# A hybrid decoder layer on one core: the feed-forward weight blocks multiplied in narrower pieces of columns

## The chip, the cores and the metric

One core of a Trainium2 chip runs the whole layer in one launch. The metric is device microseconds of that core for one execution, from the first to the last instruction with the launch around it; a small number is good. The core has a matrix engine (PE), whose weight loads are recorded as a row of their own (PEld), a vector engine (DVE), a scalar engine (ACT), a general engine (POOL) and a queue that issues transfers (SP).

## The reference

One decoder layer on 512 tokens of width 1024, all in float32: a half-step SwiGLU feed-forward block, a mixer, a second feed-forward block of the same shape, and a last normalisation. The change touches only the two feed-forward blocks. With `h` the normalised and modulated input (512 x 1024) each of them computes

```
x = x + 0.5 * gate * ((silu(h @ w_gate) * (h @ w_up)) @ w_down)
```

with `w_gate` and `w_up` of 1024 x 2816 and `w_down` of 2816 x 1024. The mixer between them (a gated convolution beside sparse attention, with one input and one output projection) is computed by the same helper, but at widths that the change leaves alone.

## The kernel before, in words

**Layout.** Everything is kept transposed: a tile has 128 channels on the partitions and the 512 tokens along the columns. `DK` = 8 tiles make the model width, `FK` = 22 tiles the hidden width, taken in two halves of `FH` = 11.

**Three products for one.** A float32 matrix is split into a high part and a low part, both in the engine's fast float32 form (`whi`, `wlo` for weights, `hhi`, `hlo` for the input, `ghi`, `glo` for the hidden layer). A product of a 128 x 128 block of weights with a 128 x 512 tile is three passes: high weights by high input, high weights by low input, low weights by high input. `mm3` (line 280) writes these. Where tile and bank are 512 wide it does the columns in `HALVES`, two pieces of 256: the three passes on the first half, then the three on the second. So one step of one block is six matmuls of 256 columns. Every matmul in the instruction stream brings its own weight load of 128 x 128.

**The feed-forward stage.** `ffn` (line 586) runs `main` (line 637) once for each block. The first three hidden tiles (`GRP` = 3) are computed by `first_group` or `first_products`, by halves of the tokens, as the input is built. For each of the other 19 hidden tiles `project` (line 542) is called twice, once for the gate block and once for the up block: 8 steps each, accumulated in one bank of 512 columns. Then `glu` (line 599) applies the gate with ACT and DVE and splits the result into `ghi`, `glo`. After the first 11 hidden tiles `part` (line 617) multiplies the down blocks of the first half: 8 output tiles of 11 steps over all 512 columns. After the last 11 hidden tiles come 6 output tiles of 11 steps over all columns, and then the last two output tiles by halves of the tokens, so that the normalisation behind them can begin early; in these the bank slice is 256 wide.

**The order of the work.** A planner written in the kernel (`Plan`) puts the instructions of all engines in order when the program is built. Each step tells it an estimated time: `c_mm3(T)` for a full step of `project` and of `part`. The order on each engine is then fixed in the program, and semaphores hold it together. Weights come over the SP queue in units of 512 KB into four buffers (`raw`), ACT makes the high part (line 372) and DVE or POOL the low part (line 361). During the first feed-forward block the same queue also brings the conditioning matrix (`araw`), which DVE sums (line 871); a few small matmuls of PE reduce those sums in `ada_reduce`.

**Elsewhere.** In the mixer `project` computes 14 blocks of the input projection in halves. The attention has matmuls of other widths with the same 128 x 128 loads: `scores` (line 1311 on) multiplies query tiles with keys of 128 to 512 columns, first with all 128 rows (`ks,q`) and then with 64 (`kl,q`); `compressed` multiplies query tiles with 64 columns (`kcs,q`).

Of the kernel before, what the change touches and what calls it, by code (L numbers as in the profile page):

```python
# [20 lines left out]
T = 512  # L21
D = 1024
DK = D // P
F = 2816
FK = F // P
FH = FK // 2
# [109 lines left out]
class Plan:  # L136
# [12 lines left out]
    def go(self, rank, task):  # L149
        self.n += 1  # L150
        self.step([rank, self.n, task, [self.at], None], None)
# [8 lines left out]
    def give(self, slots, i, at=None):  # L160
        slots.idle.append((*(at or self.at), i))
        able = [w for w in slots.waiters if w[4] < len(slots.idle)]
        if able:
            w = min(able, key=lambda w: w[:2])
            slots.waiters.remove(w)
            self.step(w, self.take(slots, w))
# [52 lines left out]
def c_act(n):  # L219
    return ACT, 0.1 + 0.84e-3 * n  # L220


def c_tt(n):
    return DVE, 0.07 + 1.04e-3 * n


def c_stt(n):
    return DVE, 0.13 + 1.04e-3 * n
# [14 lines left out]
def c_mm3(n):  # L243
    return PE, 3 * max(n / 2370, 0.105)
# [11 lines left out]
def tile_hymba_layer(ctx: ExitStack, tc: tile.TileContext, xT, pos, cols_d, con_d, wa0, wa1, f1a, f1b, f1d,  # L256
# [9 lines left out]
    HALVES = (slice(0, T // 2), slice(T // 2, T))  # L266

    bank_of = [ps.tile([P, T], F32, name=f"b{i}") for i in range(8)]
# [8 lines left out]
    def mm(o, lhsT, rhs, start, stop):  # L277
        nc.tensor.matmul(o, lhsT, rhs, start=start, stop=stop)  # L278

    def mm3(o, w, x_, start, stop):  # L280

        n = o.shape[-1]
        wide = n == T and x_[0].shape[-1] == T
        halves = HALVES if wide else (slice(0, n),)
        for ts in halves:
            x0, x1 = (x_[0][:, ts], x_[1][:, ts]) if wide else x_
            o_ = o[:, ts] if wide else o
            mm(o_, w[0], x0, start and ts is halves[0], False)
            mm(o_, w[0], x1, False, False)
            mm(o_, w[1], x0, False, stop and ts is halves[-1])  # L290


    col = const.tile([P, N_COLS], F32, name="col")
# [84 lines left out]
    def take_unit():  # L378
        used[0] += 1
        return used[0] - 1  # L380

    def cols(u, j, n=P):
        i = w_at[u]
        return whi_of[i][:, j * n:(j + 1) * n], wlo_of[i][:, j * n:(j + 1) * n]

    def free_unit(u):
        give(slots_of.get(u, ws), w_at[u])
# [128 lines left out]
    def h_of(d, ts=FULL):  # L516
        return hhi[d][:, ts], hlo[d][:, ts]
# [17 lines left out]
    def residual(d, b, gate, ts, norm):  # L535
        n = ts.stop - ts.start
        yield c_stt(n)
        nc.vector.scalar_tensor_tensor(x[d][:, ts], bank_of[b][:, ts], gate, x[d][:, ts], op0=OP.mult, op1=OP.add)  # L538
        give(banks, b)
        yield from norm.add(d, ts)  # L540

    def project(b):

        u = take_unit()
        yield made[u]
        for d in range(DK):
            yield c_mm3(T)
            mm3(bank_of[b], cols(u, d), h_of(d), d == 0, d == DK - 1)
        free_unit(u)

    def start_builds(s, norm):
# [15 lines left out]
    def first_group(order, built, accs, end, n_cols=2 * GRP):  # L567

        uses = {}
        for n, (i, d) in enumerate(order):  # L570
            yield built[i, d]
            if d not in uses:
                uses[d] = take_unit()
            yield made[uses[d]]
            ts = HALVES[i]
            for j in range(n_cols):
                if n == 0:
                    accs[j] = yield banks
                yield c_mm3(T // 2)
                mm3(bank_of[accs[j]][:, ts], cols(uses[d], j), h_of(d, ts), n == 0, n == len(order) - 1)  # L580
            if i == 1:
                free_unit(uses[d])
        done(end)


    def ffn(s, gp, accs, norm, end):
        ghi = [gp.tile([P, T], F32R, name=f"ghi{k}") for k in range(FH)]
        glo = [gp.tile([P, T], F32R, name=f"glo{k}") for k in range(FH)]
        sg_of = [gp.tile([P, T], F32, name=f"sg{k}") for k in range(2)]
        for k in range(KEEP[s]):  # L590
            whi_of.append(gp.tile([P, UNIT], F32R, name=f"whik{k}"))
            wlo_of.append(gp.tile([P, UNIT], F32R, name=f"wlok{k}"))
            give(kept[s], len(whi_of) - 1)
        sgs, gs = Slots(range(2)), [Slots([k]) for k in range(FH)]
        g_in = [Event() for _ in range(FK)]
        gate = [mod[:, 3 * s + 2, d:d + 1] for d in range(DK)]
        at = {}

        def glu(f, bg, bu):
            k = yield sgs  # L600
            yield c_act(T)
            nc.scalar.activation(sg_of[k], bank_of[bg], AF.Silu)
            give(banks, bg)
            q = yield scr
            yield c_tt(T)
            nc.vector.tensor_mul(scr_of[q], sg_of[k], bank_of[bu])  # L606
            give(banks, bu)
            give(sgs, k)
            j = yield gs[f % FH]
            yield c_act(T)  # L610
            nc.scalar.activation(ghi[j], scr_of[q], AF.Copy)  # L611
            yield c_tt(T)
            nc.vector.tensor_sub(glo[j], scr_of[q], ghi[j].bitcast(F32))  # L613
            give(scr, q)
            done(g_in[f])

        def part(half, d, b, ts, keep=False):
            for k in range(FH):
                n = d * FH + k
                if (half, n // 8) not in at:  # L620
                    at[half, n // 8] = take_unit()
                u = at[half, n // 8]
                yield made[u]
                yield g_in[half * FH + k]
                yield c_mm3(ts.stop - ts.start)
                mm3(bank_of[b][:, ts], cols(u, n % 8), (ghi[k][:, ts], glo[k][:, ts]), k == 0, k == FH - 1)
                if n % 8 == 7 and not keep:
                    free_unit(u)
                if half == 0 and d == DK - 1:
                    give(gs[k], k)  # L630

        def first_half(d, b):
            yield c_stt(T)
            nc.vector.scalar_tensor_tensor(x[d], bank_of[b], gate[d], x[d], op0=OP.mult, op1=OP.add)
            give(banks, b)

        def main():
            for f in range(GRP):
                go(R_GLU, glu(f, accs[2 * f], accs[2 * f + 1]))
            for f in range(GRP, FK):  # L640
                if f == FH:
                    for d in range(DK):
                        b = yield banks
                        yield from part(0, d, b, FULL)
                        if d == 0:
                            yield mod_in[3 * s + 2]
                        go(R_X, first_half(d, b))
                bg = yield banks
                yield from project(bg)
                bu = yield banks  # L650
                yield from project(bu)
                go(R_GLU, glu(f, bg, bu))
            for d in range(DK - 2):
                b = yield banks
                yield from part(1, d, b, FULL)
                go(R_X, residual(d, b, gate[d], FULL, norm))
            for ts in HALVES:
                for d in (DK - 2, DK - 1):
                    b = yield banks
                    yield from part(1, d, b, ts, True)  # L660
                    go(R_X, residual(d, b, gate[d], ts, norm))
            for n in range(8, FH):
                free_unit(at[1, n])
            done(end)

        go(R_MAIN, main())


    start = ctx.enter_context(ExitStack())
# [298 lines left out]
    with ExitStack() as mixer:  # L968
# [620 lines left out]
        def fill():  # L1589
            for n, f in enumerate(FILL):  # L1590
                if f == "val":
                    yield from value_products()
                elif f == "cmp":
                    yield from compressed_hidden()
                else:
                    b = yield banks.spare(FILL_SPARE)
                    yield from project(b)
                    receive(f, b, scr, n)
            done(h_done)
# [3 lines left out]
        n = 0  # L1603
# [295 lines left out]
```

## Time and profile before

| | |
|---|---|
| Time of the runs shown | median 1066.27 us of three (1066.21, 1066.27, 1082.69) |
| The profiled execution's own time | 1077.18 us |
| Its span, first to last instruction | 1075.4 us |
| PE busy | 1054.2 us, 98% of the span, 8753 matmuls and 8753 weight loads |
| DVE, ACT, POOL busy | 606.0, 408.7, 51.2 us |
| Granted PE clock, mean | 0.991 of full speed |
| Read from HBM | 130.14 MB |

The profile comes from one execution; its own time is 10.9 us over the median of the runs. A matmul's recorded time is the time from its start to its modelled end, and matmuls overlap, so the time that one takes from the engine is read from the distance between the starts of two that follow each other, or from their number in a stretch of time. The first feed-forward block lies between 24 and 409 us of the span (its down blocks at 164 to 228 and 348 to 409 us), the mixer between 409 and 697 us, the second feed-forward block from there to 1066 us (down blocks at 815 to 877 and from 1002 us).

### The profile page before, as it was taken

What the parts mean: (1) busy time and instruction counts of PE and PEld (TensorE: products, weight loads), DVE (VectorE), ACT (ScalarE), POOL (GpSimd) and SP (SyncE); (2) the same over time, 40 slices, a digit from 0 to 9 for tenths busy, and PEclk for the clock granted to TensorE, in tenths of its full rate; (3) what the DMA queues carried; (4) which work ended last, traced back from release to release, by engine and by line L of the source; (5) the groups of instructions that cost most, each with busy time, mean ns of one, the idle gap of its engine ahead of it and who ended that gap; (6) DMA issues with size and microseconds to landing.
All of it is one profiled execution on the core that took longest, in us unless ns stands there. A gap on an engine that the chain in (4) does not pass through costs nothing.

```text
span 1075.4 us, 20561 instructions
## 1 busy us (share of the span) xinstructions
PE 1054.2 (98%) x8753; PEld 1009.8 (94%) x8753; DVE 606.0 (56%) x1069; ACT 408.7 (38%) x713; POOL 51.2 (5%) x47
## 2 busy tenths in 40 slices
PE   8999999999999999999999999999999999999997
PEld 5899999999999999998887789999999999999997
DVE  4988888833333347699787786744333333233334
ACT  4552222222222224458566775333222122222321
POOL 0310100000000001021001010000000000000000
PEclk8999999999999999999999999999999999999999
DMA  9669999422232231344201014133233322322202
GB/s 336 250 217 324 326 322 323 150 99 99 99 99 99 93 89 48 122 125 160 80 18 37 1 29 130 45 118 118 83 95 99 98 84 94 99 99 85 93 21 79
DMA packets 40732, 134.02 MB, mean 125 GB/s; under 512 B 4704, under 2 KB 8032, under 8 KB 40000
## 3 DMA queue, kind: packets, MB, share of 16 engines
q1 hardware_dynamic: 40640, 132.71, 37.0%
q8 instruction: 68, 1.11, 0.4%
q14 instruction: 24, 0.20, 0.1%
HBM read 130.14 MB, written 2.10 MB: 123 GB/s over the span
## 4 chain that ended last, share of the span: by engine, by line
PE 80%; DVE 10%; DMA 6%; issue 2%; ACT 1%; SPq 0%; DVEq 0%; ACTq 0%
PE b L278 77%; DMA araw<-in_wa_dram 6%; DVE ada L871 3%; PE b L1402 2%; DVE wlo L361 2%; DVE afirst L742 1%; DMA wfirst<-in_wa_dram 1%; DVE glo L613 1%; DVE s L525 1%; ACT whi L372 0%; PE b L1297 0%; DVE s L1045 0%; DVE s L606 0%; DVE swp L1048 0%; DVE afirst L739 0%
## 5 line engine op out<-in xcount | busy, mean ns | idle before, releaser
L278 PE MATMUL b<-hhi,whi 128*128 128x256 f32 x1824 | 515.8, 283 | 0.0
L278 PE MATMUL b<-hlo,whi 128*128 128x256 f32 x1824 | 509.2, 279 | 0.6 <-DVE hlo L531 0.6
L278 PE MATMUL b<-hhi,wlo 128*128 128x256 f32 x1824 | 508.7, 279 | 0.0
L372 ACT ACTIVATE whi<-raw 128x1024 fp32r<-128x1024 f32 (+3 forms) x176 | 178.2, 1013 | 461.4 <-issue 250.3
L278 PEld LDWEIGHTS b<-hhi,whi 128*128 128x128 f32 x1824 | 343.3, 188 | 7.6 <-issue 6.7
L278 PEld LDWEIGHTS b<-hlo,whi 128*128 128x128 f32 x1824 | 346.5, 190 | 1.1 <-DVE hlo L531 1.0
L278 PEld LDWEIGHTS b<-hhi,wlo 128*128 128x128 f32 x1824 | 343.5, 188 | 0.0
L361 DVE TENSOR_TENSOR wlo<-raw,whi 128x1024 fp32r<-128x1024 f32 (+3 forms) x162 | 191.1, 1180 | 223.8 <-ACT whi L372 223.5
L278 PE MATMUL b<-ghi,whi 128*128 128x256 f32 x672 | 188.0, 280 | 0.0
L278 PE MATMUL b<-ghi,wlo 128*128 128x256 f32 x672 | 187.3, 279 | 0.0
L278 PE MATMUL b<-glo,whi 128*128 128x256 f32 x672 | 187.3, 279 | 0.0
L278 PEld LDWEIGHTS b<-glo,whi 128*128 128x128 f32 x672 | 127.6, 190 | 0.0
L278 PEld LDWEIGHTS b<-ghi,whi 128*128 128x128 f32 x672 | 126.2, 188 | 0.8 <-issue 0.8
L278 PEld LDWEIGHTS b<-ghi,wlo 128*128 128x128 f32 x672 | 126.3, 188 | 0.0
L606 DVE TENSOR_TENSOR s<-sg,b 128x512 f32<-128x512 f32 x44 | 30.0, 685 | 102.1 <-PE b L278 101.4
L871 DVE SCALAR_TENSOR_TENSOR ada<-araw,cact,ada 128x1024 f32<-128x1024 f32 x49 | 63.5, 1296 | 16.8 <-DMA araw<-in_wa_dram 16.2
L361 POOL TENSOR_TENSOR wlo<-raw,whi 128x768 fp32r<-128x768 f32 (+2 forms) x14 | 32.2, 2299 | 213.5 <-ACT whi L372 213.5
L538 DVE SCALAR_TENSOR_TENSOR x<-b,mod,x 128x512 f32<-128x512 f32 (+1 forms) x30 | 19.1, 643 | 40.8 <-PE b L278 40.7
L456 ACT ACTIVATE s<-x 128x256 f32<-128x256 f32 (+1 forms) x41 | 19.4, 491 | 54.8 <-DVE x L538 52.8
L611 ACT ACTIVATE ghi<-s 128x512 fp32r<-128x512 f32 x44 | 27.1, 620 | 15.5 <-DVE s L606 15.5
L529 ACT ACTIVATE hhi<-s,mod 128x256 fp32r<-128x256 f32 (+1 forms) x42 | 20.9, 534 | 31.2 <-DVE s L525 25.6
L613 DVE TENSOR_TENSOR glo<-s,ghi 128x512 fp32r<-128x512 f32 x44 | 32.1, 734 | 0.0
(238 smaller groups left out, 963.7 us busy)
## 6 DMA issues: line engine op xcount, KB each, us to landing
araw<-in_wa_dram SPq DMA_DIRECT2D x56, 512.0 KB
raw<-in_f1b_dram SPq DMA_DIRECT2D x38, 512.0 KB
raw<-in_f2b_dram SPq DMA_DIRECT2D x38, 512.0 KB
raw<-in_f1d_dram SPq DMA_DIRECT2D x22, 512.0 KB
raw<-in_f2d_dram SPq DMA_DIRECT2D x22, 512.0 KB
raw<-in_wib_dram SPq DMA_DIRECT2D x14, 512.0 KB
wfirst<-in_wa_dram SPq DMA_DIRECT2D x5, 1024.0 KB
raw<-in_wc_dram SPq DMA_DIRECT2D x8, 512.0 KB
```

The source lines that it names most:

```text
L278: nc.tensor.matmul(o, lhsT, rhs, start=start, stop=stop)
L361: (nc.vector if e == DVE else nc.gpsimd).tensor_sub(wlo_of[j][:, :n], raw_of[i][:, :n], whi_of[j][:, :n].bitcast(F32))
L372: nc.scalar.activation(whi_of[j][:, :n], raw_of[raw_at[u]][:, :n], AF.Copy)
L456: nc.scalar.activation(o[:, ts], x[d][:, ts], AF.Square)
L525: nc.vector.scalar_tensor_tensor(t, x[d][:, ts], am[:, s, d:d + 1], rb(), op0=OP.mult, op1=OP.mult)
L529: nc.scalar.activation(hhi[d][:, ts], t, AF.Identity, bias=sh)
L538: nc.vector.scalar_tensor_tensor(x[d][:, ts], bank_of[b][:, ts], gate, x[d][:, ts], op0=OP.mult, op1=OP.add)
L606: nc.vector.tensor_mul(scr_of[q], sg_of[k], bank_of[bu])
L611: nc.scalar.activation(ghi[j], scr_of[q], AF.Copy)
L613: nc.vector.tensor_sub(glo[j], scr_of[q], ghi[j].bitcast(F32))
L871: nc.vector.scalar_tensor_tensor(a, w, cact[:, k:k + 1], a, op0=OP.mult, op1=OP.add)
L1402: nc.tensor.transpose(pt[:, w:w + P], Pr[t][:, kb * P:(kb + 1) * P], ident)
```

## The change

`mm3` takes the pieces of columns as an argument. The gate blocks and everything in the mixer keep two pieces of 256 columns. The up blocks get three pieces of 176, 168 and 168 columns. The down blocks that run over all 512 columns get four pieces of 128. The down blocks that run by halves of the tokens keep one piece of 256, since the helper cuts only what is 512 wide. The times told to the planner are not changed.

```diff
+    def cut(*edges):
+        return tuple(slice(a, b) for a, b in zip((0,) + edges, edges + (T,)))
+
+    THIRDS, QUARTERS = cut(176, 344), cut(128, 256, 384)
+
-    def mm3(o, w, x_, start, stop):
+    def mm3(o, w, x_, start, stop, pieces=HALVES):
         n = o.shape[-1]
-        wide = n == T and x_[0].shape[-1] == T
-        halves = HALVES if wide else (slice(0, n),)
-        for ts in halves:
-            x0, x1 = (x_[0][:, ts], x_[1][:, ts]) if wide else x_
-            o_ = o[:, ts] if wide else o
-            mm(o_, w[0], x0, start and ts is halves[0], False)
-            mm(o_, w[0], x1, False, False)
-            mm(o_, w[1], x0, False, stop and ts is halves[-1])
+        if n != T or x_[0].shape[-1] != T:
+            pieces = (slice(0, n),)
+        for ts in pieces:
+            x0, x1 = x_[0][:, ts], x_[1][:, ts]
+            mm(o[:, ts], w[0], x0, start and ts is pieces[0], False)
+            mm(o[:, ts], w[0], x1, False, False)
+            mm(o[:, ts], w[1], x0, False, stop and ts is pieces[-1])
...
-    def project(b):
+    def project(b, pieces=HALVES):
...
-            mm3(bank_of[b], cols(u, d), h_of(d), d == 0, d == DK - 1)
+            mm3(bank_of[b], cols(u, d), h_of(d), d == 0, d == DK - 1, pieces)
...
-                mm3(bank_of[b][:, ts], cols(u, n % 8), (ghi[k][:, ts], glo[k][:, ts]), k == 0, k == FH - 1)
+                mm3(bank_of[b][:, ts], cols(u, n % 8), (ghi[k][:, ts], glo[k][:, ts]), k == 0, k == FH - 1, QUARTERS)
...
                 bu = yield banks
-                yield from project(bu)
+                yield from project(bu, THIRDS)
```

## Rows read from the trace of the kernel before

**Rows 1.** The page's busy times: busy us, share of the span, instructions.
```profile
PE 1054.2 (98%) x8753; PEld 1009.8 (94%) x8753; DVE 606.0 (56%) x1069; ACT 408.7 (38%) x713; POOL 51.2 (5%) x47
```

**Rows 2.** The page's chain that ended last, share of the span by engine.
```profile
PE 80%; DVE 10%; DMA 6%; issue 2%; ACT 1%; SPq 0%; DVEq 0%; ACTq 0%
```

**Rows 3.** The chain in order of time: start us, us, what.
```profile
696.36 364.83 PE b L278 x3098
```

**Rows 4.** Waits of PE, whole span: us in total, times, longest us.
```profile
PE b L278 <- DVE ada L871: 4.5, 5, 1.3
```

**Rows 5.** Stretches: us, busy us (instructions) by engine, granted clock, DMA share, GB/s.
```profile
core 0: us, PE busy (x) PEld busy (x) DVE busy (x) ACT busy (x) POOL busy (x), PEclk, DMA share, GB/s
60.00:200.00 140.00, 135.12 (x1194) 130.93 (x1194) 116.84 (x125) 41.08 (x56) 6.17 (x2) 1.00 0.87 306
220.00:330.00 110.00, 110.00 (x973) 110.00 (x972) 37.61 (x40) 30.29 (x38) 0.00 (x0) 1.00 0.29 98
340.00:390.00 50.00, 50.00 (x444) 50.00 (x443) 19.85 (x22) 14.99 (x19) 0.00 (x0) 1.00 0.35 111
700.00:810.00 110.00, 110.00 (x937) 110.00 (x936) 41.78 (x51) 35.52 (x48) 0.00 (x0) 1.00 0.35 106
815.00:870.00 55.00, 55.00 (x469) 55.00 (x468) 17.89 (x19) 11.13 (x11) 0.00 (x0) 1.00 0.29 89
```

**Rows 6.** Groups by shape: count, busy us, mean ns, idle before.
```profile
L278 PE MATMUL b<-ghi,whi 128*128 128x256 f32 x672 | 188.0, 280 | 0.0
L278 PE MATMUL b<-ghi,whik 128*128 128x256 f32 x32 | 9.2, 288 | 0.0
...
L278 PEld LDWEIGHTS b<-hlo,whi 128*128 128x128 f32 x1824 | 346.5, 190 | 1.1 <-DVE hlo L531 1.0
L278 PEld LDWEIGHTS b<-hhi,whi 128*128 128x128 f32 x1824 | 343.3, 188 | 7.6 <-issue 6.7
```

**Rows 7.** Order of time, matmuls and then loads, first feed-forward block: start us, us, what.
```profile
299.98 0.28 PE L278 MATMUL b<-hhi,wlo 128*128 128x256 f32 x1
300.09 0.28 PE L278 MATMUL b<-hhi,whi 128*128 128x256 f32 x1
...
299.98 0.19 PEld L278 LDWEIGHTS b<-hhi,whi 128*128 128x128 f32 x1
300.09 0.19 PEld L278 LDWEIGHTS b<-hlo,whi 128*128 128x128 f32 x1
```

**Rows 8.** Order of time, matmuls of the mixer at 526 to 528 us.
```profile
526.43 0.49 PE L1402 MATMUL b<-con,P 128*128 128x128 f32 x3
526.75 0.27 PE L1402 MATMUL b<-con,ssum 128*128 128x128 f32 x1
526.86 0.38 PE L1402 MATMUL b<-con,P 128*128 128x128 f32 x2
527.08 0.27 PE L1402 MATMUL b<-con,ssum 128*128 128x128 f32 x1
527.11 1.06 PE L278 MATMUL b<-kcs,q 128*128 128x64 f32 x8
528.00 0.36 PE L278 MATMUL b<-hhi,whi 128*128 128x256 f32 x1
528.20 0.28 PE L278 MATMUL b<-hlo,whi 128*128 128x256 f32 x1
528.32 0.28 PE L278 MATMUL b<-hhi,wlo 128*128 128x256 f32 x1
```

**Rows 9.** Order of time, matmuls of the attention scores at 628 us.
```profile
628.26 0.38 PE L278 MATMUL b<-kl,q 64*128 64x256 f32 x1
628.57 0.33 PE L278 MATMUL b<-ks,q 128*128 128x128 f32 x1
628.83 0.32 PE L278 MATMUL b<-kl,q 64*128 64x128 f32 x1
629.09 0.38 PE L278 MATMUL b<-hhi,whi 128*128 128x256 f32 x1
```

## Prediction

> **What bounds the kernel now.** I read the busy times first. PE is busy 98% of the span, and every matmul has its own weight load, 8753 of each [rows 1]. DVE, at 56%, is the next. A busy PE can still be waiting, so I read the chain that ended last: 80% of it is PE [rows 2], and its longest piece is one unbroken run of 364.83 us and 3098 matmuls that covers nearly the whole second feed-forward block [rows 3]. The waits confirm it: the largest wait of PE on another engine is 4.5 us in five places, for the conditioning sums of the first block [rows 4]. So time added to PE in the feed-forward blocks goes onto the end nearly one for one.
>
> The next view counts matmuls in stretches, which gives the distance from one to the next [rows 5]. In the first block that is 110 / 973 = 0.1131 us in the projections and 50 / 444 = 0.1126 us in the down blocks; in the second block 110 / 937 = 0.1174 and 55 / 469 = 0.1173 us. The granted clock is 1.00 throughout, the upper level of 2.4 GHz, at which 256 columns at one a cycle would be 0.107 us. The columns alone nearly explain the pace. But the loads run at the same pace: each begins as a matmul begins, and the next pair follows 0.11 us later [rows 7]. At 256 columns the two are so close that this stretch can't say which binds. The change decides on just that, so I looked for narrower matmuls with the same 128 x 128 loads.
>
> They are in the mixer. Eight matmuls of only **64 columns** take from 527.11 to 528.00 us, 0.89 / 8 = 0.111 us each, and right behind them those of 256 columns follow at 0.12 us [rows 8]. A quarter of the columns saves under a tenth of the time. Six matmuls of 128 columns ahead of them (transposes in full float32) take 0.65 / 6 = 0.108 us each [rows 8]. A matmul that brings its own load of 128 columns thus costs about 0.111 us however narrow it is. The columns are not what is slow: in the attention scores, where the loads alternate between 128 and 64 rows and start only after the matmul before, 256 columns take 0.31 us (628.26 to 628.57) and 128 columns 0.26 us (628.57 to 628.83, and again to 629.09) [rows 9]. The difference, 0.05 us for 128 columns, is one column a cycle at 2.4 GHz. So 128 columns stream in about 0.053 us, and the load, which takes twice that, is hidden behind 256 columns and not behind fewer.
>
> **The change part by part.** *Up blocks.* 19 in each feed-forward block, 8 steps each, 152 steps. A step goes from 6 matmuls with 6 loads to 9 with 9, at the same 1536 columns. The pieces of 168 and 176 columns lie between the rows at 64 columns (0.111 us) and at 256 (0.113 to 0.117 us); I take 0.111, since the columns would need only 0.073 us. First block: 9 x 0.111 - 6 x 0.1131 = 0.320 us, times 152 = 48.7 us. Second: 0.999 - 0.704 = 0.295 us, times 152 = 44.8 us.
>
> *Down blocks.* 8 + 6 = 14 output tiles over all columns with 11 steps each, 154 steps in each feed-forward block. The remaining two tiles go by halves and are untouched: 154 x 2 + 2 x 11 x 2 = 352 matmuls of each kind in a block, and 704 = 672 + 32 are in the trace [rows 6]. A step goes from 6 to 12 matmuls. First block: 12 x 0.111 - 6 x 0.1126 = 0.656 us, times 154 = 101.1 us. Second: 1.332 - 0.704 = 0.628 us, times 154 = 96.7 us.
>
> *Gate blocks, mixer, planner.* The gate blocks and the mixer's 14 projection blocks keep their pieces: nothing. The planner is told the same times, so the order on each engine, and each queue, SP's and POOL's included, stays as it is. No transfer, conversion or wait is added. ACT, DVE and the weight transfers work inside the longer PE time; they would have to become slower than PE to count, and DVE's 116.8 us of 140 in its densest stretch [rows 5] gets more room.
>
> *What can be given back.* The wait of 4.5 us for the conditioning sums [rows 4] lies where PE becomes slower and the transfers do not. It can go entirely, or stay where DVE's fixed order makes the sums late along with PE: 0 to -4.5, I take -3 us. What is late next there is PE itself.
>
> *Sum.* 48.7 + 44.8 + 101.1 + 96.7 - 3 = +288 us. Against the profiled execution's own 1077.2 us that is 1365 us. Its time is 10.9 us above the median of 1066.3. An estimate of why: the second block runs 3098 matmuls at 0.1178 us [rows 3] where the first has 0.1131 for the same code, 14 us in all; if the median run has the shorter pace in both, its second block pays as the first does, 2 x 149.8 - 3 = +297 us, and 1066.3 + 297 = 1363 us. If the 10.9 us lie elsewhere it is 1066.3 + 288 = 1354 us. I take **1363 us**.
>
> *Bounds.* The new pieces are 2 x (152 x 9 + 154 x 12) = 6432 matmuls. At the 0.108 us of the transposes, the low end, 19 us less: 1335. At the pace that each block has now (0.113 and 0.1174), the high end, 6 + 21 us more on 1365: 1392. The value is nearer to the row of 64 columns, whose operands are of the same kind.
>
> A rule that speaks against the change stands in the Trainium skill, "TensorE: Matmul & The Clock Gate", section "LDWEIGHTS (loading the stationary operand)": a load takes its columns divided by 1.2 in nanoseconds. For 128 columns that is 0.1067 us, where the rows have 0.111; at that pace for each new piece the sum would be 6432 x 0.0043 = 28 us smaller, about 1335 us. The rows are measured here, so the sum above keeps theirs.
>
> **The rivals.** *A, the repeated load is cheap.* In each triple the second pass uses the same high weights as the first. If a load of weights that are already in the array cost nothing, one matmul in three would go at its columns, 0.06 us, and the pieces would average (2 x 0.111 + 0.06) / 3 = 0.094 us: 6432 x 0.017 = 109 us less, about 1254 us. For it: no narrow matmul in the trace repeats its weights. Against: the repeated load (low input, high weights) is recorded 1824 times like the others, at 190 ns mean beside 188 [rows 6]. The same direction is given by the Trainium skill, "TensorE: Matmul & The Clock Gate", section "Back-to-back issue gap": about 81 ns for each of a sustained stream of loads and matmuls of 128 columns. At that figure it would be 6432 x 0.030 = 193 us less, about 1170 us; the rows of 64 columns at 111 ns contradict it for these loads.
>
> *B, the columns bind, not the load (the other side).* The price is then 1536 columns at 0.42 ns, 0.645 us a step, plus what each matmul adds: nothing at best, 0.005 us at most (from 0.1131 against 0.107). With nothing, steps of 0.679 and 0.704 become 0.645: about 306 x (0.034 + 0.059) = 28 us less, 1038 us, 2.7% faster. With 0.005 each, up steps take 0.690 and down steps 0.705: 1066.3 + 2 x (152 x 0.011 + 154 x 0.029) = 1079 us, 1.2% slower. It decides from the point at which a load takes less than the columns of a piece, 0.053 us at 128 and 0.073 us at 176. For it: the pace of now fits the columns. Against: 64 columns at 0.111 us.
>
> *C, narrow pieces stream slowly.* 64 columns in 0.111 us could also be read as four cycles a column (0.107 us). Then 128 columns cost 0.218 us and a third 0.289 us: down steps 2.62, up steps 2.60 us instead of 0.68, 612 x 1.93 = +1180 us, about 2250 us. Against: 128 columns take 0.05 us less than 256 in the scores [rows 9]; under this reading they would take longer.
>
> That the change does not reach the blocks is excluded by the code: the operands of both calls are 512 wide.
>
> **How the numbers follow.** The forecast has 0.92: it rests on two independent rows of narrow matmuls with the same load. A has 0.03, B 0.03, C 0.02. The range is the forecast's own, from the low end to the high end of the piece's price: 1335 to 1392 us; the rivals lie outside and hold 0.08. What a measurement here can tell from no change is about 2%. Faster is the best end of B, 0.01; within 2% the rest of B, 0.02; slower is the forecast with A and C, 0.97.
>
> **What would show it.** Right: up and down stretches with matmuls 0.111 us apart and a load beginning with each, the gate blocks as now, the feed-forward blocks some 150 us longer each, the mixer as long as before, and the wait for the conditioning sums smaller. A shows as distances of 0.11, 0.06, 0.11 in each triple; B as distances of 0.06 us in the down blocks; C as 0.22 us there. The forecast is wrong if PE starts to wait for weights, or if a narrow piece costs something that neither its load nor its columns show.

## The result, and the profile after

The changed kernel takes **1362.1 us** (median of four runs, 1361.3 to 1364.9) against 1066.8 us before: a ratio of 1.2776, 95% interval [1.275, 1.2801]. The forecast was 1363 us, with a range from 1335 to 1392.

The page of the changed kernel, first its busy times as in [rows 1], then its chain by engine as in [rows 2]:

```profile
PE 1342.5 (99%) x11513; PEld 1299.2 (96%) x11513; DVE 609.5 (45%) x1069; ACT 408.3 (30%) x713; POOL 51.1 (4%) x47
...
PE 93%; DVE 4%; issue 1%; DMA 1%; ACT 1%; SPq 0%; DVEq 0%; ACTq 0%
```

11513 - 8753 = 2760 more matmuls and as many more loads; DVE, ACT and POOL do what they did. PE's share of the chain goes from 80 to 93%: the conditioning sums, which the chain of before passed through, have left it.

Stretches of the changed kernel, with the columns of [rows 5]. The first and third hold gate and up blocks in turn, the second and fourth only down blocks:

```profile
core 0: us, PE busy (x) PEld busy (x) DVE busy (x) ACT busy (x) POOL busy (x), PEclk, DMA share, GB/s
310.00:440.00 130.00, 130.00 (x1159) 130.00 (x1158) 36.18 (x39) 29.70 (x38) 0.00 (x0) 1.00 0.25 78
450.00:540.00 90.00, 90.00 (x808) 90.00 (x808) 20.80 (x24) 14.81 (x18) 0.00 (x0) 1.00 0.17 55
1100.00:1240.00 140.00, 140.00 (x1248) 140.00 (x1247) 38.64 (x41) 32.79 (x42) 0.00 (x0) 1.00 0.23 79
1250.00:1330.00 80.00, 80.00 (x719) 80.00 (x718) 14.83 (x16) 12.89 (x17) 0.00 (x0) 1.00 0.06 21
```

In the down blocks 90 / 808 = 0.1114 us and 80 / 719 = 0.1113 us lie between matmuls of 128 columns, where [rows 5] had 0.1126 and 0.1173 us between those of 256. Halving a matmul has saved one part in a hundred in the first block. The wait for the conditioning sums [rows 4] is no longer among PE's waits. The matmuls of one down step in order of time, as in [rows 7], and the loads of the same stretch:

```profile
1000.09 0.27 PE L278 MATMUL b<-ghi,whi 128*128 128x128 f32 x1
1000.20 0.28 PE L278 MATMUL b<-glo,whi 128*128 128x128 f32 x1
1000.32 0.27 PE L278 MATMUL b<-ghi,wlo 128*128 128x128 f32 x1
1000.42 0.28 PE L278 MATMUL b<-ghi,whi 128*128 128x128 f32 x1
```
```profile
1000.03 0.19 PEld L278 LDWEIGHTS b<-ghi,whi 128*128 128x128 f32 x1
1000.14 0.19 PEld L278 LDWEIGHTS b<-glo,whi 128*128 128x128 f32 x1
1000.25 0.19 PEld L278 LDWEIGHTS b<-ghi,wlo 128*128 128x128 f32 x1
```

Every 0.11 us one load and one matmul, and the second of each triple (`glo,whi`), whose weights are those of the first, is no closer behind it than the others are.

### The profile page after: what moved, and what is told of

Read it like the earlier page. It is cut to its first block, busy times and chain, and to the rows that moved or that the text cites. A ratio compares the mean times of both kernels' runs of the same rounds, so it can differ in the third digit from the quotient of the medians.

```text
span 1359.6 us, 26081 instructions
## 1 busy us (share of the span) xinstructions
PE 1342.5 (99%) x11513; PEld 1299.2 (96%) x11513; DVE 609.5 (45%) x1069; ACT 408.3 (30%) x713; POOL 51.1 (4%) x47
## 4 chain that ended last, share of the span: by engine, by line
PE 93%; DVE 4%; issue 1%; DMA 1%; ACT 1%; SPq 0%; DVEq 0%; ACTq 0%
PE b L278 91%; PE b L1406 1%; DVE wlo L365 1%; DMA wfirst<-in_wa_dram 1%; DVE afirst L746 0%; DVE s L529 0%; PE b L1301 0%; DVE s L1049 0%; ACT whi L376 0%; DVE swp L1052 0%; DVE afirst L743 0%; DVE v L403 0%; PE b L1251 0%; DVE afirst L738 0%; ACT hhi L533 0%
## 5 line engine op out<-in xcount | busy, mean ns | idle before, releaser
L278 PE MATMUL b<-hhi,whi 128*128 128x256 f32 (+2 forms) x2128 | 595.7, 280 | 0.0
L278 PE MATMUL b<-hlo,whi 128*128 128x256 f32 (+2 forms) x2128 | 589.5, 277 | 0.6 <-DVE hlo L535 0.6
L278 PE MATMUL b<-hhi,wlo 128*128 128x256 f32 (+2 forms) x2128 | 589.5, 277 | 0.0
L278 PEld LDWEIGHTS b<-hhi,wlo 128*128 128x128 f32 x2128 | 405.1, 190 | 0.0
L278 PE MATMUL b<-ghi,whi 128*128 128x128 f32 (+1 forms) x1288 | 354.5, 275 | 0.0
L278 PE MATMUL b<-glo,whi 128*128 128x128 f32 (+1 forms) x1288 | 354.0, 275 | 0.0
L278 PE MATMUL b<-ghi,wlo 128*128 128x128 f32 (+1 forms) x1288 | 354.0, 275 | 0.0
L278 PEld LDWEIGHTS b<-ghi,whi 128*128 128x128 f32 x1288 | 247.4, 192 | 0.8 <-issue 0.8
L278 PEld LDWEIGHTS b<-ghi,wlo 128*128 128x128 f32 x1288 | 247.5, 192 | 0.0
L278 PEld LDWEIGHTS b<-glo,whi 128*128 128x128 f32 x1288 | 247.4, 192 | 0.0
```

## The experiments

**One part at a time.** The two parts of the change, each alone.

```diff
 # e1_up_only: against the changed kernel
-  mm3(bank_of[b][:, ts], ..., k == 0, k == FH - 1, QUARTERS)
+  mm3(bank_of[b][:, ts], ..., k == 0, k == FH - 1)
 # e2_down_only: against the changed kernel
-  yield from project(bu, THIRDS)
+  yield from project(bu)
```

> Up blocks in three pieces, down blocks back in two. Load theory (each matmul costs the larger of its weight load, 0.111 us, and its columns): 304 up steps gain three matmuls each, +97 us on the kernel before, about 1163 us. If the columns bound, it would stay within 10 us of 1067. If the two parts of the change hindered each other (banks, buffers), the sum of this run's gain and of the run with the down blocks alone would miss the 295 us of the whole change by more than 10 us.

> Down blocks in four pieces, up blocks back in two. Load theory: 308 steps with six matmuls more, +198 us on the kernel before, about 1266 us. If the columns bound: within 15 us of 1067.

Measured: 1159.0 us with the up blocks alone (ratio 1.0825 [1.0722, 1.0928]) and 1270.3 us with the down blocks alone (1.1862 [1.1766, 1.1958]). Over 1066.8 us these are +92.2 and +203.5 us. Their sum is 295.7 us, and the whole change's is 295.3. In seven runs beside these two the kernel before took 1064.4 to 1082.4 us, median 1069.1, and from that base the sum is 291 us; so the parts do not hinder each other by the 10 us named, and that the sums meet within half a microsecond is chance. The down blocks cost 5 us more than expected. The expected 198 us had the second block at its longer pace of 0.1173 us; with the first block's pace in both it is 2 x 101.1 = 202 us. The up blocks cost 5 us less, and the wait for the conditioning sums fits that: it is gone in that run, while 4.2 us of it stay with the down blocks alone.

**Half the load.** The changed kernel, with most down steps loading 64 of the 128 weight columns.

```diff
         for ts in pieces:
             x0, x1 = x_[0][:, ts], x_[1][:, ts]
-            mm(o[:, ts], w[0], x0, start and ts is pieces[0], False)
+            m = HD if pieces is QUARTERS and not start and not stop else P
+            mm(o[:m, ts], w[0][:, :m], x0, start and ts is pieces[0], False)
...
```

> The changed kernel, but in the down blocks of four pieces 9 of the 11 steps multiply with 64 of the 128 weight columns only (the lower half of the output tile is left out in them): same number of matmuls, same input columns, half the load. Load theory: those 252 steps of 12 matmuls go from 0.111 to about 0.06 us each (a load of 64 columns, and 128 input columns), 154 us less than the changed kernel: about 1208 us. If it is a fixed cost of each matmul (issue, decoding, two instructions) and not the load: 1362 us as the changed kernel.

Measured: 1203.4 us in one execution. The number of instructions and the columns that stream are those of the changed kernel, so it is neither a fixed cost of a matmul nor its columns that took 0.111 us. Its matmuls in a down block:

```profile
930.11 0.22 PE L278 MATMUL b<-ghi,whi 128*64 128x128 f32 x1
930.17 0.23 PE L278 MATMUL b<-glo,whi 128*64 128x128 f32 x1
930.23 0.22 PE L278 MATMUL b<-ghi,wlo 128*64 128x128 f32 x1
930.29 0.22 PE L278 MATMUL b<-ghi,whi 128*64 128x128 f32 x1
```

They stand 0.06 us apart, under loads of 64 columns. Which of the two binds now, half a load (an estimate: half of 0.111, 0.056 us) or the 128 columns, this run cannot say. Half the weight columns are also half the rows of the result, so a price of those rows is not told apart from the load's here.

**Fewer columns under the same load.** The changed kernel, with part of each down piece's columns left out.

```diff
         for ts in pieces:
+            last = ts is pieces[-1]
+            first = ts is pieces[0]
+            if pieces is QUARTERS and not start:
+                ts = slice(ts.start, ts.start + HD)
             x0, x1 = x_[0][:, ts], x_[1][:, ts]
...
```

`HD` is 64; the two runs after it have 96 and 112 in its place.

> The changed kernel, but in the down blocks of four pieces 10 of the 11 steps multiply only 64 of each piece's 128 columns (the other half is left out in them): same number of matmuls and loads, half the columns. Load theory: nothing changes, 1362 us. If the columns bind: 280 steps of 12 matmuls with 0.027 us less each, 90 us less, about 1270 us.

> As the run with 64 of 128 columns, but with 96 of each piece's 128 columns in 10 of the 11 down steps (the rest is left out). That run was to show nothing changed and instead lost the clock: at the upper level its matmuls stood 0.111 us apart, then the granted clock fell to 0.50. Load theory, if the clock stays up: 1362 us, unchanged. If the columns bind at the rate of the kernel in one piece (0.456 ns a column): 280 x 12 x 32 columns less, 49 us less, about 1313 us. If the clock falls here too: far over 1362 us, up to the 1730 of the other run.

> The same with 112 of 128 columns. Load theory with the clock up: 1362 us. Columns bind: 24 us less, about 1338 us. If the clock falls at 96 columns and not here, this run is the clean test.

Measured, one execution each: 1729.6 us with 64 columns, 1724.2 with 96, 1361.7 with 112. The first missed both theories by far. Its stretches show why:

```profile
core 0: us, PE busy (x) PEld busy (x) DVE busy (x) ACT busy (x) POOL busy (x), PEclk, DMA share, GB/s
182.00:187.00 5.00, 5.00 (x48) 5.00 (x47) 4.28 (x6) 1.58 (x2) 0.00 (x0) 1.00 0.74 211
187.00:406.10 219.10, 219.10 (x1036) 217.35 (x1036) 40.83 (x50) 12.68 (x14) 0.00 (x0) 0.50 0.16 51
410.00:550.00 140.00, 140.00 (x1248) 140.00 (x1247) 38.19 (x41) 32.79 (x42) 0.00 (x0) 1.00 0.25 79
```

The down blocks begin at 182.4 us. At 187 us the granted clock has fallen from 1.00 to 0.50, from 2.4 to 1.2 GHz, and it stays there to the end of the first half's down blocks at 406.1 us; in the gate and up blocks from 410 us it is 1.00 again. At the upper level the matmuls of 64 columns stood 0.11 us apart, as the load theory has it:

```profile
183.87 0.28 PE L278 MATMUL b<-ghi,wlo 128*128 128x64 f32 x1
183.98 0.28 PE L278 MATMUL b<-ghi,whi 128*128 128x64 f32 x1
184.09 0.28 PE L278 MATMUL b<-glo,whi 128*128 128x64 f32 x1
184.21 0.28 PE L278 MATMUL b<-ghi,wlo 128*128 128x64 f32 x1
```

At the lower one it is 219.10 / 1036 = 0.2115 us, 1.9 times the distance in the changed kernel's blocks. The run with 96 columns has 200 / 945 = 0.2116 us there, so the columns do not count at the lower level either, and it is the load that takes 1.9 times as long. The Trainium skill, "TensorE: Matmul & The Clock Gate", section "Part 1: The HAM clock gate (the "warmup" mystery)", says that the clock follows how busy the engine has been. Here it fell while the profile has PE and its loads busy without a gap, so a row at 100% was no sign here that the clock would stay up. In the run with 96 columns it falls in the same way, to 0.50 between 200 and 400 us. With 112 it holds, and that is the clean test:

```profile
980.00:1090.00 110.00, 110.00 (x987) 110.00 (x987) 18.84 (x19) 10.69 (x11) 0.00 (x0) 1.00 0.15 52
```

110 / 987 = 0.1114 us, the pace of 128 columns, and 1361.7 us in all, not 1338: the columns don't count there.

**One wide piece.** Everything that is 512 wide in one piece, half the loads of the kernel before.

```diff
-    THIRDS, QUARTERS = cut(176, 344), cut(128, 256, 384)
+    THIRDS, QUARTERS = cut(), cut()
...
-    def mm3(o, w, x_, start, stop, pieces=HALVES):
+    def mm3(o, w, x_, start, stop, pieces=(FULL,)):
...
-    def project(b, pieces=HALVES):
+    def project(b, pieces=(FULL,)):
```

> All blocks that are 512 wide (gate, up, down, and those of the mixer's projections) in one piece: three matmuls of 512 columns a step, half the loads of the kernel before. If a load still costs something at 256 columns (one column a cycle, 0.213 us for 512, and 0.005 us a matmul), a step goes from 0.68 to 0.65 us and the 1076 such steps save 26 us: about 1041 us, faster than both. If at 256 columns the columns alone bind, at the pace of the attention's matmuls of 512 columns (0.224 to 0.237 us each), a step stays at 0.67 to 0.70 us: 1060 to 1085 us, no gain from fewer loads.

Measured: 1083.3 us, ratio 1.0122 [1.0045, 1.02]. The time lies in the second range: halving the loads gains nothing. Two stretches of it, projections and down blocks:

```profile
240.00:350.00 110.00, 110.00 (x473) 88.60 (x473) 37.35 (x40) 30.50 (x39) 0.00 (x0) 1.00 0.29 95
360.00:400.00 40.00, 40.00 (x173) 32.24 (x172) 16.17 (x18) 11.92 (x15) 0.00 (x0) 1.00 0.36 111
```

110 / 473 = 0.2326 us for 512 columns, 0.454 ns a column; PEld is idle a fifth of the time for once. One column a cycle would be 0.213 us. What takes the other 0.02 us was not tried. At 0.454 ns a column 256 columns would take 0.116 us; the kernel before has 0.113 us there in one stretch and 0.117 in another [rows 5]. So whether the load or the columns bind at 256 stays open, and the run shows only that fewer loads gain nothing.

**Uneven pieces.** As many loads, matmuls and columns as the kernel before, in pieces of 128 and 384.

```diff
-    THIRDS, QUARTERS = cut(176, 344), cut(128, 256, 384)
+    THIRDS, QUARTERS = cut(176, 344), cut(128)
...
-                yield from project(bu, THIRDS)
+                yield from project(bu)
```

> Down blocks in two uneven pieces, 128 and 384 columns, up blocks in two of 256: as many matmuls, loads and columns as the kernel before. If only one load can be ahead, under the running matmul, a step is 3 x 0.111 + 3 x 0.170 = 0.84 us instead of 0.68: +51 us, about 1117 us. If loads can run further ahead, the short and the long matmuls average out and the time stays at 1067 us.

Measured: 1123.0 us, ratio 1.0481 [1.0392, 1.057]. So time does not follow the sums of loads and columns, which are unchanged, but matmul by matmul the larger of the two: a long matmul does not lend its spare time to the loads of the short ones. A whole step takes 860.69 - 859.83 = 0.86 us:

```profile
859.83 0.39 PE L278 MATMUL b<-ghi,whi 128*128 128x384 f32 x1
860.06 0.34 PE L278 MATMUL b<-glo,whi 128*128 128x384 f32 x1
860.24 0.34 PE L278 MATMUL b<-ghi,wlo 128*128 128x384 f32 x1
860.41 0.22 PE L278 MATMUL b<-ghi,whi 128*128 128x128 f32 x1
860.47 0.27 PE L278 MATMUL b<-glo,whi 128*128 128x128 f32 x1
860.58 0.28 PE L278 MATMUL b<-ghi,wlo 128*128 128x128 f32 x1
860.69 0.39 PE L278 MATMUL b<-ghi,whi 128*128 128x384 f32 x1
```

With 0.454 ns a column, 3 x 0.111 + 3 x 0.174 = 0.86 us. The start of the second short matmul stands only 0.06 us behind the first and that of the second long one 0.23 us; the sum of a step is sound, a single distance at a change of width is not. The loads of the same step are plainer:

```profile
859.88 0.19 PEld L278 LDWEIGHTS b<-glo,whi 128*128 128x128 f32 x1
860.06 0.19 PEld L278 LDWEIGHTS b<-ghi,wlo 128*128 128x128 f32 x1
860.24 0.19 PEld L278 LDWEIGHTS b<-ghi,whi 128*128 128x128 f32 x1
860.41 0.19 PEld L278 LDWEIGHTS b<-glo,whi 128*128 128x128 f32 x1
860.52 0.19 PEld L278 LDWEIGHTS b<-ghi,wlo 128*128 128x128 f32 x1
860.63 0.19 PEld L278 LDWEIGHTS b<-ghi,whi 128*128 128x128 f32 x1
860.75 0.19 PEld L278 LDWEIGHTS b<-glo,whi 128*128 128x128 f32 x1
```

Three distances of 0.17 to 0.18 us from load to load, then three of 0.11 to 0.12: no load gets ahead by more than one matmul.

**The kernel before, once more.** No edit.

> The kernel before, unchanged, for the pace of its second feed-forward block. The prediction's estimate: an execution near 1066 us has 0.113 us from matmul to matmul there, as in the first block, and one near 1077 us has 0.1175. If the 10 us lie elsewhere, the second block has 0.1175 us in an execution near 1066 us too.

Measured: 1067.8 us in one execution. Its second feed-forward block:

```profile
700.00:800.00 100.00, 100.00 (x885) 100.00 (x884) 42.27 (x58) 35.81 (x50) 0.00 (x0) 1.00 0.34 106
815.00:870.00 55.00, 55.00 (x487) 55.00 (x487) 18.53 (x19) 11.72 (x12) 0.00 (x0) 1.00 0.30 97
```

100 / 885 = 55 / 487 = 0.113 us, where [rows 5] have 0.1174 and 0.1173. The estimate holds in this pair of executions: the 1077 us of the first profile had a slower pace in the second feed-forward block. The changed kernel's gate blocks there have the shorter pace too: eleven of their matmuls, starting from 901.28 to 902.41 us, stand 0.113 us apart. What sets the pace was not found.

## Why the prediction was right

*The bound.* PE carried the feed-forward blocks, and time added there came out at the end: 295 us.

*The price of a piece* was the step that all hung on, 0.111 us from the eight matmuls of 64 columns [rows 8]. It is 0.1114 in the down blocks. The reading was weaker than it looked: the eight stand between two changes of width, where one start says little, and of the matmuls of 256 columns that "follow at 0.12 us" the first stands 0.20 us behind them. The loads, which the prediction did not show there, bear it out:

```profile
527.08 0.97 PEld L278 LDWEIGHTS b<-kcs,q 128*128 128x128 f32 x8
527.97 0.19 PEld L278 LDWEIGHTS b<-hhi,whi 128*128 128x128 f32 x1
```

Eight of them take 527.97 - 527.08 = 0.89 us, 0.111 us each. That it is the load, and not a fixed cost or the columns, was read from the scores [rows 9] and is now shown from both sides: half the load, 0.06 us; 112 columns in place of 128, no change. The half load leaves one thing open, that the rows of the result were halved with it.

*The terms.* The stages of the execution at 1067.8 us and of the changed kernel's give them one by one. First the two pieces of their chains that hold the second feed-forward block:

```profile
700.49 351.34 PE b L278 x3098
842.69 502.63 PE b L278 x4478
```

It is 151.3 us longer, forecast 149.8 for this pace. The last piece of the chain in the first block starts 141.4 us later (at 409.67 and at 551.05 us), which is less by the waits given back below. From there to the second block it is 291 us before and 292 after, so the mixer is as long as before, as the prediction's signs have it. The down blocks of the second feed-forward block's first half last from 814.9 to 874.8 us before and from 978.0 to 1095.9 after: +58.0 us for 88 steps, 0.659 us each, where the prediction had 0.656 with both blocks at the shorter pace. The projections of hidden tiles 12 to 22 go from 119.7 to 148.5 us in the first block: +28.8 us for 88 up steps, 0.327 each, forecast 0.320. So a matmul of an up step takes 0.112 us and not 0.111.

*What was given back* was set too small: 0 to 4.5 us, taken as 3. The execution at 1067.8 us waits 6.7 us for the conditioning sums and 1.2 us more on an issue, and the changed kernel for neither. The two misses cancel: 304 x 0.327 + 308 x 0.659 - 7.9 = 294.5 us, against 1361.3 - 1067.8 = 293.5 in these two executions. That the forecast lies within 1 us of the result is luck; that it lies within some 10 us is not.

*The base.* The forecast came from the estimate that a median run has the shorter pace in both blocks. The repeated run bears it out; without it the sum would have been 1354 or 1365. Its 14 us are more than the 9.4 us between the two spans; the execution at 1067.8 us waits some 3 us longer for the sums and on an issue.

*The rivals.* A fails on the trace after: the repeated load is paid in full, no distance of 0.06 us in a triple. B fails on the runs with half the load and with 112 columns, C on the pace of 0.111 at 128 columns. Two figures in rival B were off. What a matmul adds, 0.1131 against 0.107, is 0.006 us and not 0.005, which makes its slow end about 1085 us, still far outside the range. And in the wide piece a column takes 0.45 ns, not the 0.42 of one a cycle; the 0.073 us for the columns of a third becomes 0.08, under the load's 0.111 either way, so the sum does not change.

## What to carry to other kernels

A matmul that brings its own load of 128 weight columns, in the fast float32 form of this kernel, costs at least 0.111 us here at a granted clock of 1.00, measured with 64, 112 and 128 columns. An estimate from that and 0.45 ns a column: pieces under some 250 columns are paid as if they had that many. Price a cut by the number of pieces, and look for the narrowest matmuls with the same loads in the trace before making it. Judge each piece by itself: wide pieces don't pay for narrow ones. And from 256 to 512 columns fewer loads gained nothing.

## What was not expected of the hardware

Narrow pieces can cost the clock. With 96 or 64 columns under each load of 128 the granted clock fell to 0.50 in the down blocks, though PE and PEld stood at 100% busy, and every matmul there went from 0.111 to 0.21 us: one execution each, 363 and 368 us more than with 112 columns, where it stayed at 1.00. With 128 columns every 0.06 us under half loads it stayed up as well. Why it fell was not tried further.
